# A SwiGLU block's gate and up products: weights as the moving operand, with a block scheme of seven products for eight over halves of the contraction

## The chip, the cores and the metric

The kernel runs on one core of one Trainium2 chip. The metric is the device time of one execution in microseconds (us). The kernel before takes 2006.88 us, the median of three runs (2005.92 to 2008.11). All arrays are fp32 in DRAM.

## What is computed

One inference step of a backbone layer over 128 context tokens and 256 latent tokens with D = 2048 channels: a modulation from a conditioning vector (six vectors of 2048, each for two conditions), a mixing sub-layer, and a SwiGLU feed-forward network (FFN) with 5632 hidden units. The change touches the FFN and what lies around it:

```
mod = silu(cond) @ w_ada + b_ada          # six vectors; ga2 is the last ("modulation 5")
...
h  = rmsnorm(x, norm_pre_ffn) * (1 + sc2) + sh2
ff = (silu(h @ w_ffn_gate) * (h @ w_ffn_up)) @ w_ffn_down
x  = x + ga2 * rmsnorm(ff, norm_post_ffn)
```

h is 384 tokens x 2048, gate and up are 2048 x 5632, down is 5632 x 2048.

## The kernel before

**Numbers.** Every fp32 operand is split into two parts, hi (a cast to the matmul's fp32r format) and lo (the difference), and a product takes three matmuls: w_hi x_hi, w_lo x_hi, w_hi x_lo. An operand is on chip as a pair of tiles: whi and wlo for weights, A_hi and A_lo (`h2`) for h, hid_hi and hid_lo for the hidden units.

**Weights.** A weight arrives in pieces of 512 KB, 128 partitions x 1024. SyncE (SP) issues the load into one of two buffers `raw` (L1307) or into four resident buffers `uraw` (tiles u012 and u3s, L1301). `split_next` (L1318) lets ScalarE (ACT) cast it to whi (L1324) and VectorE (DVE) subtract for wlo (L1325). There are four buffers each of whi and wlo. The list `ready` holds three pieces ahead of TensorE; `grab2` (L1336) takes the first, issues loads (`load_more`, L1289), splits one more piece, and issues one deferred VectorE operation out of the list `pend` (two in the last chunk).

**The FFN.** It goes through 11 chunks of 512 hidden units, `FC` = 4 column tiles each. Per chunk, gate and up take 16 pieces: `proj2` (L1374) takes two pieces for a column tile of 128, with the weights as the stationary operand and h as the moving one, 384 columns (`gemm`, L277; 24 matmuls a piece, 384 in a chunk). SiLU of gate is ScalarE's (L1349), the product with up VectorE's (L1356, tile hfE), and hid is split by `split_act` (L303, L304). The hidden units so stand with channels on partitions, which is how the down product needs them as its stationary operand.

The down product of chunk c runs inside chunk c + 1, in two halves (`down`, L1391). w_d is the moving operand, 512 columns. Per half, the context tokens are multiplied plainly and the latent tokens by a scheme of seven products for eight on blocks of 2 x 2: VectorE forms sums of four pieces of w_d (`combine`, L1312) and of hid (L1362 to L1367, once in a chunk), and TensorE makes 66 matmuls (`wmm`, L1386), 132 in a chunk. Nine partial results of 512 columns per half are added into fp32 sums in SBUF (psums, `unit`), L1408, by copies of ScalarE in the first chunk (L1406). In the last chunk the down product is plain (kind "e", tile pde).

**PSUM.** Two pools hold one bank (128 x 512) per buffer: psm with three ("mm"), used by gate and up, and pss with five ("side"), used by down.

**Modulation 5.** `ada_rest` (L563) works through w_ada for one modulation: per half of its columns, 16 loads of 512 KB (adaw, two buffers), each followed by a multiply (L573) or multiply-add (L575) on VectorE for each of two conditions, 1024 columns; then eight small matmuls (pr, L583), a copy by ScalarE (adev, L588), two transposes (ptm, L592) and small VectorE operations. It is a generator; `paced` and `step` let it take 0.25 of a step at each piece of gate and up, and what remained before the last piece would be finished there (L1478).

**The tail.** For the last norm, `add_last` (L1442) adds the last sums and squares them with a sum per token. `diagonal` (L1492) puts the factors 1/rms on a diagonal for each of three token tiles; `turn` (L1508, matmul L1512) turns blocks of f by a matmul with that diagonal, which scales and transposes at once; then x1 + ga2 x f is formed (L1537, or L1529 and L1530) and stored.

**What sets the order.** Each engine executes its instructions in the order in which the program emits them, and waits at one whose inputs or buffer are not ready. The lists above (`ffn_order`, `pend`, `ready`) and the pace of the modulation decide that order; the pools put the waits.

Of the kernel before, what the change touches and what calls it, by code (L numbers as in the profile page):

```python
# [96 lines left out]
def tile_step(ctx: ExitStack, tc: tile.TileContext, a, o):  # L97
# [74 lines left out]
    ffn_order = []  # L172
    for c in range(NFC):
        for j in range(FC):
            ffn_order.append(("g", c, j))
            if c and j == FC - 1 and c < NFC - 1:
                ffn_order.append(("d", c - 1, 1))
            ffn_order.append(("u", c, j))
            if c == NFC - 1 and j == FC - 1:
                ffn_order.append(("d", c - 1, 1))  # L180
            if c and j == 1:
                ffn_order.append(("d", c - 1, 0))
    ffn_order += [("e", NFC - 1, n) for n in (0, 2, 1, 3)]
# [5 lines left out]
    def ffn_srcs(kind, c, j):  # L189
        if kind == "d":  # L190

            return [("U", 0, down_src(c, j, 0)), ("U", 1, down_src(c, j + 2, 0)), ("U", 2, down_src(c, j + 2, 1)),
                    ("U", 3, down_src(c, j, 1)), ("T", 0), ("T", 1), ("T", 2), ("T", 3)]
        if kind == "e":
            return [("E", down_src(c, j, kh)) for kh in range(2)]
        return two(a["w_" + kind], c * FC + j)

    first = [ffn_srcs(*u) for u in ffn_order[:HEAD]]
    srcs += [f[g] for g in range(2) for f in first]
    ffn_items = []  # L200
    for u in ffn_order[HEAD:]:
        ffn_items += ffn_srcs(*u)

    plain = 2 * (2 * FC - HEAD)
    srcs += ffn_items[:plain]
    ffn_items = ffn_items[plain:]
# [834 lines left out]
    with ExitStack() as s:  # L1041
# [3 lines left out]
            pe.tile([P, FC, T], F32R, tag=f"hid_{n}", name=f"hid_{n}") for n in ("hi", "lo")  # L1045
        )
        pd_stack = s.enter_context(ExitStack())
# [39 lines left out]
        spare_h = ((pe, "hid_hi", 2), (pe, "hid_lo", 2))  # L1087
        spare_w = ((adap, "adaw", 2), (adap, "adaw", 2))
        raw2 = None
        for i in range(KT):  # L1090
            p = psm.tile([P, T], F32, tag="mm", name="pmm")
            for g in range(2):
# [3 lines left out]
                else:  # L1096
# [9 lines left out]
                    if -4 <= n <= -2:  # L1106
                        split(spare_w if n == -3 else spare_h)
# [150 lines left out]
        for q in range(2):  # L1258
# [10 lines left out]
        chi = actp.tile([P, 3, G], F32, tag="C_hi", name="u012")  # L1269
        clo = actp.tile([P, 3, G], F32, tag="C_lo", name="u3s")  # L1270
        uraw = [chi[:, 0], chi[:, 1], chi[:, 2], clo[:, 0]]
        S = [pf.tile([P, FC, TL], F32R, name=f"S_{n}") for n in ("hi", "lo")]
        units = [t[:, n, :] for t in (
            actp.tile([P, 6, 512], F32, tag="B_hi", name="psums"), actp.tile([P, 6, 512], F32, tag="B_lo", name="psums"),
            pf.tile([P, 2, 512], F32, name="psums2"),
        ) for n in range(t.shape[1])]
        units += [clo[:, 1 + n // 2, 512 * (n % 2) : 512 * (n % 2) + 512] for n in range(4)]

        def unit(j, x):

            return units[9 * j + x]

        entries, busy = list(raws), [False]
        raws.clear()
        entries = [("R", e[0]) for e in entries]
        items = [("R", src) for _, src in srcs] + [x if isinstance(x, tuple) else ("R", x) for x in ffn_items]
        pend, late_sums = [], [True]

        def load_more():  # L1289
            n = 0  # L1290
            while items and n < 3:
                it = items[0]
                if it[0] == "T":
                    entries.append(it)
                    items.pop(0)
                    continue
                if it[0] == "U":
                    if it[1] == 0 and busy[0]:
                        return
                    busy[0] = True  # L1300
                    SP.dma_start(uraw[it[1]].rearrange("p (i x) -> p i x", i=2), it[2])  # L1301
                    entries.append(("R", uraw[it[1]]))
                else:
                    if sum(e[0] == "R" and not any(e[1] is u for u in uraw) for e in entries) >= 2:
                        return
                    raw = wp.tile([P, G], F32, tag="raw", name="raw", bufs=2)
                    SP.dma_start(raw.rearrange("p (i x) -> p i x", i=2) if it[0] == "E" else raw, it[1])  # L1307
                    entries.append(("R", raw))
                items.pop(0)
                n += 1  # L1310

        def combine(n):  # L1312

            w11, w12, w22, w21 = uraw
            (lambda: DVE.tensor_sub(w22, w22, w12), lambda: DVE.tensor_sub(w12, w12, w11),  # L1315
             lambda: DVE.tensor_add(w11, w11, w22), lambda: DVE.tensor_sub(w21, w21, w11))[n]()  # L1316

        def split_next():  # L1318
            if not entries:
                return  # L1320
            e = entries.pop(0)
            raw = e[1] if e[0] == "R" else uraw[(2, 1, 0, 3)[e[1]]]
            hi, lo = (wp.tile([P, G], F32R, tag=t, name=t, bufs=4) for t in ("whi", "wlo"))
            ACT.copy(hi, raw)  # L1324
            DVE.tensor_sub(lo, raw, hi.bitcast(F32))  # L1325
            ready.append((hi, lo))

            if raw is uraw[2] and e[0] == "R":
# [293 lines left out]
```

## Time and profile before

| | |
|---|---|
| Median of three runs | 2006.88 us (2005.92 to 2008.11) |
| The profiled execution: its own time | 2006.71 us |
| its span in the profile | 2004.9 us |
| Instructions in the span | 29287 |
| FFN in the span, from the first matmul of gate and up (L1246) to the last of w_d | 906.0 to 1987.6 us |

The profiled execution's time exceeds its span by what lies before the first and after the last instruction of the trace. Busy time of TensorE is given for matmuls (PE) and for loading the stationary operand (PEld) apart, and overlaps between neighbours. A row of the timeline gives start, length, engine, line, operation and tiles; a row of waits gives who waited for whom, the sum in us, how many times and the mean; a row of the windows gives the stretch, its length, busy time with the count for PE, PEld, DVE, ACT and POOL, then the granted TensorE clock, the share of DMA and GB/s; a row of DMA gives the tile and its source, the queue, the count, the size and the median us from issue to landing; a row of groups gives line, engine, operation, tiles, shapes and count, then busy us and mean ns, then idle time before.

### The profile page before, as it was taken

To read this page: it belongs to the slowest core of one execution; us is meant where nothing else is said; L and a number is where in the kernel's file an instruction comes from. 1 tells how busy PE (TensorE), PEld (TensorE's weight loads), DVE (VectorE), ACT (ScalarE), POOL (GpSimd) and SP (SyncE) were. 2 spreads that over 40 slices of the span, in tenths; PEclk is the share of its full clock that TensorE was granted. 3 is DMA by queue.
4 is the path that set the end of the run, shared out by engine and by line. 5 is a ranking of instruction groups with operands and counts; after the bars stand their busy time and mean duration, and the time that the engine had idled before them with its cause. 6 is when DMAs were issued, how large, how long until landed. Compare 5 with 4: busy or idle time off the path is not lost.

```text
span 2004.9 us, 29287 instructions
## 1 busy us (share of the span) xinstructions
PE 1987.6 (99%) x11652; PEld 1868.2 (93%) x11652; DVE 1481.5 (74%) x1887; ACT 852.7 (43%) x1220; POOL 32.2 (2%) x44
## 2 busy tenths in 40 slices
PE   8999999999999999999999999999999999999998
PEld 5779999999999999999999998989998989899997
DVE  5668798888667778867566868776868686767676
ACT  4233454544346554446344434343434333343333
POOL 0000000000000000003000000000000000000001
PEclk9999999999999999999999999999999999999999
DMA  9978677767646786645435353544444454434343
GB/s 389 370 246 272 218 254 247 231 219 253 221 158 201 241 291 196 200 158 204 154 117 177 126 168 127 168 126 147 148 147 157 137 168 133 156 102 156 113 161 126
DMA packets 124521, 380.18 MB, mean 190 GB/s; under 512 B 13788, under 2 KB 32412, under 8 KB 120032
## 3 DMA queue, kind: packets, MB, share of 16 engines
q1 hardware_dynamic: 123520, 377.13, 56.9%
q8 instruction: 91, 1.49, 0.3%
q10 hardware_dynamic: 864, 1.18, 0.2%
q14 instruction: 46, 0.38, 0.1%
HBM read 361.48 MB, written 16.78 MB: 189 GB/s over the span
## 4 chain that ended last, share of the span: by engine, by line
PE 85%; DVE 11%; issue 2%; ACT 2%; DMA 1%; POOL 0%; DVEq 0%; ACTq 0%; POOLq 0%
PE pmm L277 64%; PE pdn L1386 5%; DVE wlo L1325 5%; PE pv L418 3%; DVE psums L1408 2%; PE pf L277 2%; PE pde L1386 2%; PE pgm L401 1%; ACT whi L1324 1%; PE px L436 1%; DVE u3s L1316 1%; PE pmm L1246 1%; DVE u L1315 1%; DVE adacc L575 1%; DMA raw<-in_w_g 1%
## 5 line engine op out<-in xcount | busy, mean ns | idle before, releaser
L277 PE MATMUL pmm<-A_hi,whi 128*128 128x384 f32 x2480 | 833.2, 336 | 0.0
L277 PE MATMUL pmm<-A_hi,wlo 128*128 128x384 f32 x2480 | 832.0, 335 | 0.0
L277 PE MATMUL pmm<-A_lo,whi 128*128 128x384 f32 x2480 | 830.1, 335 | 0.0
L277 PEld LDWEIGHTS pmm<-A_hi,wlo 128*128 128x128 f32 x2480 | 465.8, 188 | 4.3 <-DVE wlo L1325 4.3
L277 PEld LDWEIGHTS pmm<-A_hi,whi 128*128 128x128 f32 x2480 | 466.0, 188 | 3.8 <-issue 1.4
L277 PEld LDWEIGHTS pmm<-A_lo,whi 128*128 128x128 f32 x2480 | 465.9, 188 | 1.0
L1325 DVE TENSOR_TENSOR wlo<-raw,whi 128x1024 fp32r<-128x1024 f32 x175 | 214.2, 1224 | 214.4 <-ACT whi L1324 214.4
L1324 ACT CAST whi<-raw 128x1024 fp32r<-128x1024 f32 x175 | 183.1, 1052 | 310.9 <-DMA raw<-in_w_g 146.6
L575 DVE SCALAR_TENSOR_TENSOR adacc<-adaw,spad,adacc 128x1024 f32<-128x1024 f32 x240 | 297.1, 1279 | 0.7 <-DMA adaw<-in_w_ada 0.4
L243 ACT CAST whi<-raw 128x1024 fp32r<-128x1024 f32 x181 | 189.9, 1052 | 197.4 <-DMA raw<-in_w_gate 78.2
L244 DVE TENSOR_TENSOR wlo<-raw,whi 128x1024 fp32r<-128x1024 f32 x179 | 218.0, 1222 | 69.5 <-ACT whi L243 69.0
L1325 DVE TENSOR_TENSOR wlo<-u,whi 128x1024 fp32r<-128x1024 f32 x120 | 144.6, 1221 | 37.4 <-ACT whi L1324 36.9
L1324 ACT CAST whi<-u 128x1024 fp32r<-128x1024 f32 x120 | 125.0, 1050 | 75.5 <-PE pdn L1386 28.7
L1386 PE MATMUL pdn<-wlo,hid_hi 128*128 128x512 f32 x280 | 111.3, 398 | 3.2 <-DVE wlo L1325 2.8
L1386 PE MATMUL pdn<-whi,hid_lo 128*128 128x512 f32 x280 | 109.7, 392 | 0.0
L1386 PE MATMUL pdn<-whi,hid_hi 128*128 128x512 f32 x280 | 109.2, 390 | 0.0
L1408 DVE TENSOR_TENSOR psums<-psums,pdn 128x512 f32<-128x512 f32 x126 | 83.7, 682 | 0.0
L303 ACT CAST hid_hi<-hfE 128x384 fp32r<-128x384 f32 x44 | 22.6, 514 | 131.8 <-DVE hfE L1356 131.8
L1386 PEld LDWEIGHTS pdn<-wlo,hid_hi 128*128 128x128 f32 x280 | 52.6, 188 | 20.0 <-DVE wlo L1325 10.0
L1386 PEld LDWEIGHTS pdn<-whi,hid_hi 128*128 128x128 f32 x280 | 52.6, 188 | 11.0 <-ACT sg L1349 0.4
L1386 PE MATMUL pdn<-whi,S_hi 128*128 128x512 f32 x160 | 62.4, 390 | 0.0
L1386 PE MATMUL pdn<-wlo,S_hi 128*128 128x512 f32 x160 | 62.4, 390 | 0.0
(327 smaller groups left out, 2182.7 us busy)
## 6 DMA issues: line engine op xcount, KB each, us to landing
adaw<-in_w_ada SPq DMA_DIRECT2D x128, 512.0 KB, 4.1
raw<-in_w_g SPq DMA_DIRECT2D x88, 512.0 KB, 4.4
raw<-in_w_u SPq DMA_DIRECT2D x88, 512.0 KB, 4.5
slab<-in_w_ada SPq DMA_DIRECT2D x32, 1024.0 KB
raw<-in_w_gate SPq DMA_DIRECT2D x64, 512.0 KB, 4.5
u<-in_w_d SPq DMA_DIRECT2D x60, 512.0 KB, 4.4
raw<-in_w_in SPq DMA_DIRECT2D x44, 512.0 KB, 3.6
raw<-in_w_out SPq DMA_DIRECT2D x32, 512.0 KB, 4.5
```

What stands on the lines that cost most here:

```text
L243: ACT.copy(hi, raw)
L244: sub = lambda: eng.tensor_sub(lo, raw, hi.bitcast(F32))
L277: PE.matmul(dst, w[wi][:, k * n + n0 : k * n + n0 + P], x[xi][:, k0 + k, :], start=first and k == 0 and j == 0, stop=last and k == kts - 1 ...
L303: ACT.copy(hi, src)
L401: PE.matmul(pgv[q : q + 32, :], spad[:, k, :], slab[k // (KT // 2)][:, k % (KT // 2), :], start=k < 4, stop=k >= KT - 4,)
L418: PE.matmul(pv[2 * t + g], hT[x_][:, kb, t * P : (t + 1) * P], w_[:, g * 512 : (g + 1) * 512], start=kb == 0 and j == 0, stop=kb == KT - 1 ...
L436: PE.matmul(px, w_[:, u * P : (u + 1) * P], hT[x_][:, kb, :], start=j == 0, stop=j == 2)
L575: DVE.scalar_tensor_tensor(acc[:, c, :], w, spad[:, k, c : c + 1], acc[:, c, :], op0=ALU.mult, op1=ALU.add,)
L1324: ACT.copy(hi, raw)
L1325: DVE.tensor_sub(lo, raw, hi.bitcast(F32))
L1386: PE.matmul(dst, stat[x_][:, m, :], w[w_].rearrange("p (i k c) -> p i k c", i=2, k=2)[:, :, m, :], start=first and m == 0 and n == 0, stop ...
L1408: DVE.tensor_add(unit(j, x), unit(j, x), pt[x])
```

## The change

Chunk 0 keeps gate and up as they were. From chunk 1 on (chunks 2 to 11 in the words of the change), gate and up have the weights as the moving operand, in pieces of 256 rows of the contraction by 512 columns (all four column tiles; 1 KB contiguous per row of the source), and 128 tokens x 128 rows of h as the stationary one. The three token tiles t = 0 (context), 1 and 2 (latent) are the rows of the output. The context is multiplied plainly; the latent tokens go by seven block products for eight, with the halves of the contraction and gate against up as the two block indices of the weights. The schedule of a chunk is a list of steps, four of each kind:

- **A** (up, first half of the contraction) and **B** (gate, first half) read eight resident buffers (tiles u012, u345, u67), loaded up to a chunk ahead. A makes p1 and q1, B p5 and q3.
- **C** (gate, second half) arrives in `raw`, makes q3 and p3; VectorE forms from it and the resident pieces the sums that **E** (p6) and **F** (p7) use.
- **G** (up, second half) arrives in `raw`, makes q2 and p2; **H** (p4) uses another such difference.
- **D** is w_d, now plain: eight steps for each chunk, the first four between the E's, the other four behind the H's, three token tiles each. Its banks come from psm.

A step takes one piece from `ready`; a product over a piece takes six matmuls of 512 columns. A sums operation (`sum1`, or the differences in `split_next`) stands beside the splits. The ten partial banks (`banks`, from pss) are read by `evict`; hid now comes out with tokens on partitions (g0, g1, s5), and `turn_hid` transposes it into hid's layout, 12 transposes a chunk: token tiles 0 and 1 behind step A1 of the next chunk, tile 2 behind A2, in banks of psm. `left_sums` forms the sums of h once, during chunk 0. `grab2` now issues everything in `now` and two of `pend`.

Modulation 5 becomes `ada_last`: four quarters of 512 columns, loads of 256 KB into two halves of one buffer (w5), sums in acc5. It steps at 0.8 in A, G and the last four D's, and before its small matmuls (in psm) it yields as long as `pend` is not empty or a D has its banks. What remains is finished in one loop behind step D3 of the last chunk but one's w_d (the last lines below).

In the tail, f is scaled by 1/rms first (`scale`, on ScalarE, VectorE and GpSimd), then turned by plain transposes.

```diff
+        def left_sums():
...
+            h11, h12, h21, h22 = ([f(x) for x in Hx(t, k)] for t, k in ((1, 0), (1, 8), (2, 0), (2, 8)))
...
+        for c in range(1, NFC):
+            steps += [("A", c, i) for i in range(4)] + [("B", c, i) for i in range(4)]
+            for i in range(4):
+                steps += [("C", c, i), ("E", c, i), ("D", c - 1, i)]
+            for i in range(4):
+                steps += [("F", c, i), ("G", c, i), ("H", c, i)] + ([("D", c - 1, 4 + i)] if c < NFC - 1 else [])
+        steps += [("D", NFC - 2, 4 + i) for i in range(4)]
+        d_order = (0, 2, 1, 3)
+        steps += [("D", NFC - 1, 2 * n + k) for n in d_order for k in range(2)]
+        def gu_src(kind, c, half, i):
+            return a["w_" + kind][FC * c : FC * c + FC, half, :, 256 * i : 256 * i + 256].rearrange("n p x -> p n x")
...
+        def load_more(kept=1):
+            while pairs and out_now[0] < 2:
...
+            while kept and resident:
...
+        def sum1(c, i):
+            x, y = (slots[slot(n, c, i)] for n in range(2))
+            DVE.tensor_sub(x, y, x)
...
         def split_next():
...
+            kind, c, i, raw = entries.pop(0)
+            x, y = (slots[slot(n, c, i)] if kind not in "RD" else None for n in range(2))
+            src = raw if kind in "RCGD" else y if kind == "F" else x
             hi, lo = (wp.tile([P, G], F32R, tag=t, name=t, bufs=4) for t in ("whi", "wlo"))
+            ACT.copy(hi, src)
+            if (kind, i) == ("A", 3):
+                sum1(c, 0)
+            elif kind == "B" and i < 3:
+                sum1(c, i + 1)
+            elif kind == "C":
+                DVE.tensor_sub(x, raw, x)
+                DVE.tensor_sub(y, raw, y)
+            elif kind == "G":
+                DVE.tensor_sub(x, raw, x)
+            DVE.tensor_sub(lo, src, hi.bitcast(F32))
...
+        def grab2(kept=2):
             w = take()
+            while now:
+                now.pop(0)()
+            load_more(kept)
             split_next()
+            for _ in range(2):
                 if pend:
                     pend.pop(0)()
             return w
+        def ada_last():
+            m = 5
+            acc, wt = (adap.tile([P, 2, 512], F32, tag="adaw", name=n, bufs=2) for n in ("acc5", "w5"))
+            for q in range(4):
+                for k in range(KT):
+                    w = wt[:, k % 2, :]
+                    SP.dma_start(w, a["w_ada"][m - 2, q // 2, k, :, 512 * (q % 2) : 512 * (q % 2) + 512])
...
+                    yield
+                while pend or d_live[0]:
+                    yield
+                pr = psm.tile([P, P], F32, tag="mm", name="pr")
...
+                while pend or d_live[0]:
+                    yield
+                pt = psm.tile([P, P], F32, tag="mm", name="ptm")
+                PE.transpose(pt, ev, ident)
...
+        def products(w, todo, by_tile=False):
+            order = [(x, y) for x in ((0, 1),) for y in todo] if by_tile else [((0,), y) for y in todo] + [((1,), y) for y in todo]
+            for ws, (dst, stat, mov, first, last) in order:
+                for w_ in ws:
+                    for m in range(2):
+                        for x_ in range(2 - w_):
+                            PE.matmul(
+                                dst, stat[x_][m], mov(w[w_], m),
+                                start=first and w_ == m == x_ == 0, stop=last and w_ == m == 1,
+                            )
...
+        of_kind = {
+            "A": (("p1", Hx(1, 0), True, True), ("q1", Hx(0, 0), True, True)),
+            "B": (("p5", S1, True, True), ("q3", Hx(0, 0), True, False)),
+            "C": (("q3", Hx(0, 8), False, True), ("p3", S4, True, True)),
+            "E": (("p6", S2, True, True),),
+            "F": (("p7", S3, True, True),),
+            "G": (("q2", Hx(0, 8), True, True), ("p2", Hx(1, 8), True, True)),
+            "H": (("p4", Hx(2, 8), True, True),),
+        }
...
+        def evict(c, kind):
...
+            if kind == "A":
+                now.extend([lambda: ACT.copy(s1, B["p1"]), lambda: ACT.copy(sq, B["q1"])])
+            elif kind == "B":
+                now.append(lambda: ACT.copy(s5, B["p5"]))
+            elif kind == "C":
+                pend.extend([lambda: add(g0, sq, B["q3"]), lambda: add(g1, s5, B["p3"]), lambda: silu(g0)])
...
+        def turn_hid(dst, t, pool, tag):
+            pt = pool.tile([P, FC, P], F32, tag=tag, name="ptr")
+            src = (g0, g1, s5)[t]
+            for j in range(FC):
+                PE.transpose(pt[:, j, :], src[:, j * P : (j + 1) * P], ident)
+            hi, lo = (x[:, :, t * P : (t + 1) * P] for x in dst)
+            pend.extend([lambda: ACT.copy(hi, pt), lambda: DVE.tensor_sub(lo, pt, hi.bitcast(F32))])
...
+        rate[0] = 0.8
+        ada = paced(ada_last(), rate)
...
+                if kh == 0:
+                    while pend:
+                        pend.pop(0)()
+                    pool, tag = (pss, "side") if last_c and done % 2 else (psm, "mm")
+                    pd_tiles = [pool.tile([P, 512], F32, tag=tag, name="pdn") for _ in range(3)]
+                    d_live[0] = True
...
+                products(w, todo, by_tile=last_c and kh == 1)
+                if kh == 1:
+                    if not last_c:
+                        d_live[0] = False
+                        for t in range(3):
+                            if c == 0:
+                                pend.append(lambda u=unit(t, n), p=pd_tiles[t]: ACT.copy(u, p))
+                            else:
+                                pend.append(lambda u=unit(t, n), p=pd_tiles[t]: DVE.tensor_add(u, u, p))
...
+                if i == 3:
+                    evict(c, kind)
+                if kind == "A" and c > 1 and i in (1, 2):
+                    for t in ((0, 1), (2,))[i - 1]:
+                        turn_hid(hid, t, psm, "mm")
+                if kind in "AG":
+                    step(ada)
+            if (kind, c, i) == ("D", NFC - 2, 3):
+                while pend:
+                    pend.pop(0)()
+                for _ in ada:
+                    pass
...
+            PE.transpose(py[k][:, t * P : (t + 1) * P], unit(t, k // 4)[:, (k % 4) * P : (k % 4 + 1) * P], ident)
+        scale(DVE, 0, 0)
+        scale(DVE, 0, 1)
...
+        scale(POOL, 1, 3)
```

More of the change, by code (lines that the diff above doesn't have):

```diff
@@ L1277, in tile_step @@
[L1277 to L1283, printed above, removed]
-        raws.clear()
[L1285 to L1316, printed above, removed]
+        slots = [t[:, n, :] for t, k in (
+            (actp.tile([P, 3, G], F32, tag="C_hi", name="u012"), 3), (actp.tile([P, 3, G], F32, tag="C_lo", name="u345"), 3),
+            (adap.tile([P, 2, G], F32, tag="adacc", name="u67"), 2),
+        ) for n in range(k)]
@@ new lines, in tile_step @@
+        raws.clear()
+        pairs = []
+        for _, src in srcs:
+            entries.append(["R", 0, 0, None])
+            pairs.append((entries[-1], src))
+        for kind, c, i in steps:
+            e = [kind, c, i, None]
+            entries.append(e)
+            if kind in "CGD":
+                pairs.append((e, src_of(kind, c, i)))
+        resident = [(kind, c, i) for c in range(1, NFC) for kind in "AB" for i in range(4)]
+        out_now = [sum(e[3] is not None for e in entries)]
@@ L1369, in tile_step @@
+            DVE.tensor_mul(hf, ep[j % 2][:, 0:T], p)
+            split_act(hid[0][:, j, :], hid[1][:, j, :], hf)
         dst_of = {"g": gate_dst, "u": up_dst}
@@ L1372, in tile_step @@
             dst_of[kind](hp[u], c, j)
[L1374 removed]
+        n = 0
+        for kind, c, j in ffn_order[HEAD:]:
             p = psm.tile([P, T], F32, tag="mm", name="pmm")
             for g in range(2):
[L1377 to L1389 removed]
```

365 lines of the change are left out of this document (189 added, 176 removed).

## Prediction

> **What bounds the kernel now.** First the page of the profile: the span, TensorE's share, the chain.
>
> ```profile
> span 2004.9 us, 29287 instructions
> ...
> PE 1987.6 (99%) x11652; PEld 1868.2 (93%) x11652; DVE 1481.5 (74%) x1887; ACT 852.7 (43%) x1220; POOL 32.2 (2%) x44
> ...
> PE 85%; DVE 11%; issue 2%; ACT 2%; DMA 1%; POOL 0%; DVEq 0%; ACTq 0%; POOLq 0%
> ```
>
> TensorE (PE) is never free and most of the chain is its own, so an edit is worth what it does to TensorE's stream. Durations of matmuls overlap; what counts is start to start, from the timeline of PE, first and last of a run each time: 43 intervals at 512 columns, 40 at 384, and the final turns (128 columns, plain fp32) in one row.
>
> ```profile
> 1403.31 0.39 PE L1386 MATMUL pdn<-whi,hid_lo 128*128 128x512 f32 x1
> ...
> 1413.06 0.39 PE L1386 MATMUL pdn<-whi,hid_hi 128*128 128x512 f32 x1
> ...
> 1416.93 0.34 PE L277 MATMUL pmm<-A_hi,wlo 128*128 128x384 f32 x1
> ...
> 1423.86 0.34 PE L277 MATMUL pmm<-A_hi,whi 128*128 128x384 f32 x1
> ...
> 1989.86 6.52 PE L1512 MATMUL py<-dg,psums 128*128 128x128 f32 x56 [0.19 <-DVE dg L1494]
> ```
>
> So 0.2267 us, 0.1733 us and 0.116 us. The length of a chunk comes from one VectorE (DVE) line that runs once in each (instructions of the tile hfE), its slack from a stretch of 100 us, and PE's waits from the waits of PE's loads after 960 us.
>
> ```profile
> L1362 DVE TENSOR_TENSOR hfE<-hfE x10: 424/425/426, 975.6 to 1862.1; 128x256 f32<-128x256 f32 x10
> ```
>
> ```profile
> 1210.00:1310.00 100.00, 98.95 (x523) 91.82 (x522) 76.47 (x81) 37.47 (x42) 0.00 (x0) 1.00 0.46 148
> ```
>
> ```profile
> PEld pdn L1386 <- DVE wlo L1325: 10.2, 17, 1.1
> PEld pmm L277 <- DVE wlo L1325: 4.3, 17, 0.3
> ```
>
> A chunk takes (1862.1 - 975.6) / 9 = 98.5 us; its stream is 384 x 0.1733 + 132 x 0.2267 = 96.5 us. VectorE is busy 76 us of 100, and TensorE waits only some 15 us for it in the whole FFN. The FFN is bound by TensorE with little slack on VectorE.
>
> **The change: TensorE's stream.** For c = 1 to 10 the 384 matmuls of gate and up become 11 products x 6 matmuls x 4 slices = 264 of 512 columns; the 132 of w_d become 144; and 12 turns are added. 408 x 0.2267 + 12 x 0.116 = 93.9 us against 96.5: -2.6 us a chunk, **-25.5 us** in ten. The 2.0 us by which a chunk exceeds its stream are partly waits on wlo behind the sums of w_d, which go: between 0 and -20 us; I take **-12**, what the two rows of waits mostly hold.
>
> **VectorE.** Prices, start to start, from its timeline; ScalarE's cast from the page:
>
> ```profile
> 1488.61 1.22 DVE L1325 TENSOR_TENSOR wlo<-u,whi 128x1024 fp32r<-128x1024 f32 x1
> 1489.74 2.47 DVE L575 SCALAR_TENSOR_TENSOR adacc<-adaw,spad,adacc 128x1024 f32<-128x1024 f32 x2
> 1492.13 1.22 DVE L1325 TENSOR_TENSOR wlo<-u,whi 128x1024 fp32r<-128x1024 f32 x1
> ...
> 1504.47 2.35 DVE L1325 TENSOR_TENSOR wlo<-u,whi 128x1024 fp32r<-128x1024 f32 x2
> 1506.74 1.28 DVE L1408 TENSOR_TENSOR psums<-psums,pdn 128x512 f32<-128x512 f32 x2
> 1507.93 1.22 DVE L1325 TENSOR_TENSOR wlo<-u,whi 128x1024 fp32r<-128x1024 f32 x1
> ```
>
> ```profile
> L1324 ACT CAST whi<-raw 128x1024 fp32r<-128x1024 f32 x175 | 183.1, 1052 | 310.9 <-DMA raw<-in_w_g 146.6
> ```
>
> 1024 wide (a wlo or a difference) 1.13 us; 512 wide 0.60; the multiply-add of the modulation 1.195 at 1024, so 1.195 - 0.53 = 0.66 at 512 (an estimate from these rows), a pair 1.3. A chunk now has 36 wlo, 16 differences, 27 of 512: 58.8 + 16.2 = 75 us, and up to ten pairs, 88 us, below 93.9: VectorE does not bound on the whole. But TensorE waits for it in places, and these I read from the order of the new program's instructions and what each waits for.
>
> Place 1: **the turns of hid in step A1** (c = 2 to 10). They come in TensorE's queue behind A1's matmuls and go to the three psm buffers that D's last three sums held. The second turn is released by the sum of D's tile 1, and in VectorE's queue that sum stands behind wlo of B1. There are four buffers of whi and wlo and three are ahead, so wlo(A3) can't start before D's last matmul has read its buffer. Take that end as 0. VectorE then does wlo(A3), two 512, a difference, wlo(B0), two 512, a difference, wlo(B1), one 512: 5 x 1.13 + 5 x 0.60 = 8.65 us, with starts and hand-overs 8.9. TensorE arrives after A0, A1 and four turns: 24 x 0.2267 + 0.46 = 5.9. Everything of A2 is queued behind the turn. So **3.0 us** a chunk, where no multiply-adds lie between (c = 3, 4, 7, 8). In c = 5 and 10 four pairs lie there, in 6 and 9 three: counted from wlo(A0), which starts 0.7 us after step G3 (7.4 us before 0), 9 x 1.13 + 10 x 0.60 + 8 x 0.66 = 21.5, so the gate opens at 14.3: **8.4 us**; with three pairs 7.1. In c = 2 the sums are copies by ScalarE behind its cast of B1 (1.05 us by its row): about 2. Sum 2 + 4 x 3.0 + 2 x 8.4 + 2 x 7.1 = **+45 us**; between 25 (VectorE half as late) and 60.
>
> Place 2: **the rest of the modulation.** It is paced by 0.8 at steps A, G and late D, but waits while anything is pending, and the order shows the last quarter, 16 pairs, in one block behind D(9,3), with its eight small matmuls on TensorE ahead of F(10,0). So TensorE stands through all of it; the splits that are ready don't help. w5 has two halves: a load goes out when the pair two earlier is done. What a load takes, by the DMA view (of 1110 to 1810 us, and of the end):
>
> ```profile
> adaw<-in_w_ada SPq DMA_DIRECT2D x22, 512.0 KB, 3.7
> ```
>
> ```profile
> gate<-gates_d SPq DMA_DIRECT2D x32, 192.0 KB, 3.9
> ...
> out_yT<-x1b ACTq DMA_DIRECT2D x6, 192.0 KB, 2.6
> ```
>
> And the prices of what stands around the pairs, from the groups of instructions after 940 us:
>
> ```profile
> L573 DVE TENSOR_SCALAR adacc<-adaw,spad 128x1024 f32<-128x1024 f32 x4 | 2.8, 749 | 0.0
> ...
> L583 PE MATMUL pr<-adacc,selr 128*32 128x256 f32 x32 | 2.1, 385 | 0.0
> ...
> L592 PE MATMUL ptm<-ident,adev 128*128 128x128 f32 x4 | 0.8, 270 | 0.0
> L588 ACT COPY adev<-pr 128x256 f32<-128x256 f32 x2 | 0.7, 373 | 1.1 <-PE pr L583 1.1
> ```
>
> 256 KB lies between 192 and 512 KB: 2.8 us by the line through 2.6 and 3.7, and 3.9 at most. Two pairs then take 2.8 + 0.1 + 1.3 = 4.2; seven such 29.5; the first two pairs 0.8 (half of 749 ns, twice) + 1.3 = 2.1. Ahead stand the third quarter's three sums (1.8), matmuls (0.4), copy (0.4) and transpose (0.3), 3.0 us; behind, matmuls, copy and transpose again, 1.1, and as much for hand-overs, 2.1. **+37 us**; 26 at VectorE's own pace (15 x 1.3 + 0.8 + 5), 45 with loads of 3.9 us. Before, such operations lay singly in VectorE's slack and their last one started at 1737 us:
>
> ```profile
> L575 DVE SCALAR_TENSOR_TENSOR adacc<-adaw,spad,adacc x240: 1275/1279/1292, 158.1 to 1737.2; 128x1024 f32<-128x1024 f32 x120
> ```
>
> After a pause the clock matters. The granted clock, and busy counts, by windows, and TensorE's last row:
>
> ```profile
> 4.00:8.00 4.00, 3.84 (x6) 2.19 (x7) 0.71 (x2) 3.47 (x8) 0.00 (x0) 1.00 1.00 407
> 8.00:14.00 6.00, 6.00 (x17) 3.37 (x16) 5.97 (x13) 5.08 (x12) 0.00 (x0) 1.00 1.03 418
> ...
> 2000.00:2004.90 4.90, 0.00 (x0) 0.00 (x0) 0.00 (x0) 0.00 (x0) 0.00 (x0) 0.86 0.56 198
> ```
>
> ```profile
> 1998.67 0.39 PE L1512 MATMUL py<-dg,u3s 128*128 128x128 f32 x2
> ```
>
> The first matmuls take 0.64 us, later ones 0.35: half speed for about 6 us from the start. At the end 0.86 means half speed for 1.4 us, so the clock fell at about 2003.5, some 4.5 us after the last matmul. So +3 after place 2; in place 1 the pauses are 4.6 us at most, and I count nothing. The Trainium skill's page "TensorE: Matmul & The Clock Gate", section "What's actually happening", halves the clock after an idle window of about 3.4 us and restores it after as much work: then each of the four chunks with pairs would lose some 1.7 us more. No row here shows a pause that short.
>
> Small ones, together **+3** (0 to 6). Before the last D the hid is turned, cast and split, and the last tile's part has nothing to cover it:
>
> ```profile
> L304 DVE TENSOR_TENSOR hid_lo<-hfE,hid_hi 128x384 fp32r<-128x384 f32 x43 | 24.0, 558 | 24.9 <-ACT hid_hi L303 24.9
> ...
> L303 ACT CAST hid_hi<-hfE 128x384 fp32r<-128x384 f32 x43 | 22.1, 514 | 131.2 <-DVE hfE L1356 131.2
> ```
>
> At 384 columns cast and difference take 1.1 us, at 512 some 1.5. The tail scales twelve blocks where three diagonals were made, on three engines at once, another 1.5. Nothing for the sums of h at c = 0: 14 wide operations, 14 x 1.13 = 16 us, in VectorE's slack there, 13.6 us of the last 26 of chunk 0 and as large a share of the 19 before; without it, 16.
>
> ```profile
> 950.00:976.00 26.00, 26.00 (x152) 26.00 (x151) 12.40 (x13) 6.93 (x9) 0.00 (x0) 1.00 0.55 179
> ```
>
> Nothing for loads in pieces of 1 KB: no row has them in the FFN. Pieces of 4 KB and of 2 KB land alike:
>
> ```profile
> raw<-in_w_g SPq DMA_DIRECT2D x56, 512.0 KB, 4.4
> u<-in_w_d SPq DMA_DIRECT2D x45, 512.0 KB, 4.4
> ```
>
> A load has from wlo two loads earlier to its own step, some 6.8 us; late by 1 us each, 80 loads would cost 80, which I hold improbable.
>
> **Sum.** -25.5 - 12 + 45 + 37 + 3 + 3 = +50.5 us on the execution profiled, 2006.7 us (span 2004.9, 0.2 below the median of 2006.88): **2057 us**.
>
> **Rivals.**
> 1. The gates of place 1 open in time. For it: ready weights lie three steps ahead and VectorE has 19 us of slack a chunk. Against: its queue is in order and the sum stands behind wlo(B1). Without the 45: 2012 us.
> 2. Pauses of place 1 halve the clock, twice a chunk with pairs, 3 us each by the row of the start: +24, 2081 us. For it: 4.6 us against the 4.5 of the end. Against: turns lie between.
> 3. Faster: TensorE's own stream decides, because VectorE reaches what TensorE stands before in time, the block of place 2 too. Price: -25.5 - 12 + 3 = -34.5, 1972 us. It decides the sign only if all waits together stay below 34.5 us, of 85 counted; the block alone at VectorE's pace has 26. Against: the multiply-adds can't precede their loads.
> 4. The change doesn't do what it says: the order shows all 2640 and 1584 matmuls at 512 columns. 2007 us.
>
> **Numbers.** The forecast with its bounds 0.72; rival 1 0.10; rival 2 0.10; rival 3 0.07; rival 4 0.01. The range 2030 to 2083 takes in the forecast's bounds that don't all fall together and rival 2, and leaves out 1, 3 and 4. Differences below 0.2% can't be told from no change here; faster 0.07, same 0.02 (rival 4 and a part of 1), slower 0.91.
>
> **What would show it.** PE busy falls from 99%; at turns of hid idle time released by VectorE's psums line, 3 us without and 7 to 8 us with multiply-adds; one pause near 37 us in the last chunk, released by a multiply-add, which itself waits for in_w_ada; between turns, a chunk near 94 us of stream. It is wrong if that pause is missing or short, if the turns wait below 1 us, or if pgu matmuls are paced otherwise than 0.227 us.

## The result, and the profile after

| | before | after |
|---|---|---|
| median | 2006.78 us (2005.92 to 2008.11, 4 runs) | 2094.74 us (2092.76 to 2096.18, 4 runs) |
| ratio, 95% interval | | 1.0437 (1.0419 to 1.0455) |
| span of the profiled execution | 2004.9 us | 2094.4 us |

The changed kernel is 88 us slower. The sign was forecast; the size (+50) was not, and the time lies above the range of 2030 to 2083 us. The page of the changed kernel, its span, busy times and chain:

```profile
span 2094.4 us, 27765 instructions
...
PE 1980.6 (95%) x10676; PEld 1744.8 (83%) x10676; DVE 1628.7 (78%) x2048; ACT 903.6 (43%) x1261; POOL 33.2 (2%) x44
...
PE 83%; DVE 10%; DMA 4%; ACT 2%; issue 2%; SPq 0%; POOL 0%; DVEq 0%; ACTq 0%; POOLq 0%
```

TensorE has lost 7 us of busy time and gained 97 us of idle time (2004.9 - 1987.6 = 17 before, 2094.4 - 1980.6 = 114 now). Where the idle time lies, the waits of PE's matmuls say, from chunk 2 to the last product (who waited for whom, the sum, how many times, and the longest single wait, not the mean, as was said of these rows above):

```profile
PE ptr L1524 <- DVE psums L1576: 40.7, 16, 4.7
PE pr L1415 <- DVE acc L1406: 31.1, 1, 31.1
PE pdn L1463 <- DVE psums L1576: 18.7, 9, 5.6
PE ptr L1524 <- ACT psums L1574: 2.3, 1, 2.3
...
PE ptm L1425 <- ACT adev L1420: 0.8, 2, 0.4
```

First and fourth row, 43.0 us, are the turns of hid in step A1. The second is the one block of the modulation. The third, 18.7 us, was in no term of the forecast: w_d's products wait for sums of w_d. With the small rows these are some 94 us; before, PE's matmuls waited 2.8 us from 960 us to the end of the FFN (the 15 us of the prediction are waits of its weight loads).

**Turns.** Chunk c = 3, without multiply-adds; PE, then VectorE, in the same microseconds:

```profile
1176.23 1.07 PE L1463 MATMUL pgu<-wlo,A_hi 128*128 128x512 f32 x4
1178.03 0.66 PE L1524 MATMUL ptr<-ident,ep 128*128 128x128 f32 x4 [0.73 <-DVE psums L1576]
1180.89 0.66 PE L1524 MATMUL ptr<-ident,ep 128*128 128x128 f32 x4 [2.21 <-DVE psums L1576]
```

```profile
1177.29 0.68 DVE L1576 TENSOR_TENSOR psums<-psums,pdn 128x512 f32<-128x512 f32 x1
1177.89 1.22 DVE L1353 TENSOR_TENSOR u<-u,u 128x1024 f32<-128x1024 f32 x1
1179.02 1.22 DVE L1372 TENSOR_TENSOR wlo<-u,whi 128x1024 fp32r<-128x1024 f32 x1
1180.15 1.28 DVE L1576 TENSOR_TENSOR psums<-psums,pdn 128x512 f32<-128x512 f32 x2
```

The first sum frees a bank at 1177.97 and the first turn starts; the second sum stands behind a difference and a wlo and ends at 1180.8, and the second turn starts at 1180.89. VectorE is never idle in between: it does, in order, what it was given.

**The block.** PE, and the loads of w5 in that stretch:

```profile
1959.70 0.61 PE L1463 MATMUL pdn<-wlo,hid_hi 128*128 128x512 f32 x2
...
1961.65 0.33 PE L1425 MATMUL ptm<-ident,adev 128*128 128x128 f32 x1 [0.39 <-ACT adev L1420]
1993.05 1.22 PE L1415 MATMUL pr<-acc,selr 128*32 128x128 f32 x16 [31.07 <-DVE acc L1406]
...
1994.84 0.77 PE L1463 MATMUL pgu<-whi,A_hi 128*128 128x512 f32 x1
```

```profile
w<-in_w_ada SPq DMA_DIRECT2D x14, 256.0 KB, 2.6
```

**The third row.** Step D4 of chunk 2's w_d; PE's third token tile and VectorE beside it:

```profile
1239.84 0.39 PE L1463 MATMUL pdn<-whi,hid_lo 128*128 128x512 f32 x1
1241.54 0.50 PE L1463 MATMUL pdn<-whi,hid_hi 128*128 128x512 f32 x1 [1.31 <-DVE psums L1576]
```

```profile
1236.19 1.23 DVE L1372 TENSOR_TENSOR wlo<-u,whi 128x1024 fp32r<-128x1024 f32 x1 [1.64 <-ACT whi L1362]
1237.34 1.28 DVE L1576 TENSOR_TENSOR psums<-psums,pdn 128x512 f32<-128x512 f32 x2
1238.53 1.22 DVE L1371 TENSOR_TENSOR u<-raw,u 128x1024 f32<-128x1024 f32 x1
1239.67 1.22 DVE L1372 TENSOR_TENSOR wlo<-raw,whi 128x1024 fp32r<-128x1024 f32 x1
1240.80 0.68 DVE L1576 TENSOR_TENSOR psums<-psums,pdn 128x512 f32<-128x512 f32 x1
```

It is the turns' mechanism at another place. D4 takes the three psm banks of D2 and D3; two of their sums go by themselves, the third stands behind a difference and a wlo. VectorE even had 1.64 us to spare just before.

**The clock.** Windows in c = 3 around the pause's longer part, in c = 7 over the same pause, and after the block (the column behind the five engines is the granted clock):

```profile
1178.15:1181.57 3.42, 1.21 (x9) 0.97 (x10) 3.42 (x5) 0.00 (x0) 0.00 (x0) 1.00 0.00 0
1181.57:1184.98 3.41, 3.41 (x9) 2.67 (x9) 1.00 (x1) 0.04 (x1) 0.00 (x0) 0.50 0.02 5
1184.98:1188.39 3.41, 3.41 (x18) 2.77 (x18) 1.83 (x2) 1.49 (x2) 0.00 (x0) 1.00 0.00 0
1594.58:1598.00 3.42, 2.04 (x11) 1.22 (x9) 3.42 (x5) 1.05 (x1) 0.00 (x0) 1.00 0.00 0
1598.00:1601.41 3.41, 1.86 (x10) 1.63 (x11) 3.23 (x4) 0.00 (x0) 0.00 (x0) 1.00 0.00 0
1994.00:2000.00 6.00, 5.56 (x27) 4.31 (x20) 3.95 (x6) 2.76 (x4) 0.00 (x0) 0.72 0.00 0
```

The same pause is followed by half clock and 9 matmuls in 3.41 us in c = 3, and by full clock in c = 7. The windows are steps of the grid on which this trace's clock changes: its thirteen stretches at half clock with work in them all start and end on one grid of 3.41 us, and are 1, 2, 3 or 10 steps of it long. In c = 3 the idle stretch of 2.21 us lies whole in one step, with 1.21 us of work, and the next step has half the clock. In c = 7 a boundary (1598.00) cuts it in two; both steps have 1.86 us of work or more, and the clock stays. In this trace, from 960 us to the end of the FFN, every step at full clock with 1.93 us of idle time or more was followed by half clock, and none with 1.86 or less. In other runs the grid lies elsewhere against the program, so it is partly chance which pauses cost. The forecast had taken 4.5 us as the length of a pause from which the clock falls. At the end of the kernel before, the last matmul ends at 1999.1 and the clock falls at 2003.5: between them lie the rest of a step that still had 2.4 us of work and one whole idle step, so 4.5 us was a delay and no threshold.

**The balance.** The work with hardly a wait is e13_best below, with as many instructions of TensorE and a span of 1971.1 us: 33.8 below the kernel before. From there to 2094.4 are 123.3 us: 94 are idle time of TensorE (114 against 20), as much as the rows above hold, and 29 are busy time (1980.6 against 1951.2). Of these 29, some 25 are the clock. The sum over the twelve stretches at half clock from 960 us on:

```profile
sum 98.99, PE 50.31 PEld 39.51 DVE 68.77 ACT 10.44 POOL 1.15; mean PE 4.19 PEld 3.29 DVE 5.73 ACT 0.87 POOL 0.10
```

TensorE works 50.3 us in them, and does half as much as it would at full clock (9 matmuls against 18 above). In e13_best the clock is 1.00 from 960 to 1955 us.

### The profile page after: what moved, and what is told of

It is laid out like the page before. It is cut to its first block, busy times and chain, and to the rows that moved or that the text cites. A ratio compares the mean times of both kernels' runs of the same rounds, so it can differ in the third digit from the quotient of the medians.

```text
span 2094.4 us, 27765 instructions
## 1 busy us (share of the span) xinstructions
PE 1980.6 (95%) x10676; PEld 1744.8 (83%) x10676; DVE 1628.7 (78%) x2048; ACT 903.6 (43%) x1261; POOL 33.2 (2%) x44
## 4 chain that ended last, share of the span: by engine, by line
PE 83%; DVE 10%; DMA 4%; ACT 2%; issue 2%; SPq 0%; POOL 0%; DVEq 0%; ACTq 0%; POOLq 0%
PE pmm L252 30%; PE pgu L1463 26%; PE pdn L1463 16%; PE pv L393 3%; DVE wlo L1372 2%; PE pgm L376 1%; DMA raw<-in_w_in 1%; DVE acc L1406 1%; DVE u L1353 1%; PE px L411 1%; DVE psums L1576 1%; DMA w<-in_w_ada 1%; PE pmm L1222 1%; PE ptr L1524 1%; ACT whi L218 1%
## 5 line engine op out<-in xcount | busy, mean ns | idle before, releaser
L252 PE MATMUL pmm<-A_hi,whi 128*128 128x384 f32 x1200 | 404.2, 337 | 0.0
L252 PE MATMUL pmm<-A_hi,wlo 128*128 128x384 f32 x1200 | 401.3, 334 | 0.0
L252 PE MATMUL pmm<-A_lo,whi 128*128 128x384 f32 x1200 | 401.2, 334 | 0.0
L1463 PE MATMUL pgu<-whi,A_hi 128*128 128x512 f32 x640 | 258.2, 403 | 0.0
L1463 PE MATMUL pgu<-whi,A_lo 128*128 128x512 f32 x640 | 255.7, 399 | 0.0
L252 PEld LDWEIGHTS pmm<-A_hi,whi 128*128 128x128 f32 x1200 | 225.3, 188 | 2.5 <-issue 1.4
L252 PEld LDWEIGHTS pmm<-A_lo,whi 128*128 128x128 f32 x1200 | 225.4, 188 | 0.2
L252 PEld LDWEIGHTS pmm<-A_hi,wlo 128*128 128x128 f32 x1200 | 225.3, 188 | 0.0
L1463 PE MATMUL pdn<-whi,hid_hi 128*128 128x512 f32 x480 | 190.5, 397 | 19.4 <-DVE psums L1576 18.7
L1463 PE MATMUL pgu<-wlo,A_hi 128*128 128x512 f32 x640 | 186.1, 393 | 0.0
L1463 PEld LDWEIGHTS pgu<-whi,A_hi 128*128 128x128 f32 x640 | 124.3, 194 | 26.2 <-issue 0.4
```

Of the source, the lines that this page charges most:

```text
L252: PE.matmul(dst, w[wi][:, k * n + n0 : k * n + n0 + P], x[xi][:, k0 + k, :], start=first and k == 0 and j == 0, stop=last and k == kts - 1 ...
L1463: PE.matmul(dst, stat[x_][m], mov(w[w_], m), start=first and w_ == m == x_ == 0, stop=last and w_ == m == 1,)
```

## Experiments

Times without an interval are one execution; executions of the runs with an interval differ by up to 6 us.

**e1_no_mod5** leaves out modulation 5's sums.

```diff
-        ada = paced(ada_last(), rate)
+        POOL.memset(mods[:, 5], 1.0)
+        ada = paced(iter(()), rate)
```

> Leaves out modulation 5's sums (its values are set to one), so its loads, multiply-adds and small matmuls are gone. Theory: the block behind step D3 of the last chunk but one's w_d costs 36 us, and the pairs lengthen the wait at A1's turns in c = 5, 6, 9, 10 from 3.2 us to 8 to 9, another 20, plus 3 of half clock and of D4 in c = 5: about 2036 us. Rival, the pairs only fill VectorE's slack and A1's wait is the same with and without them: 2058 us.

Measured 2023.02 us, and PE's waits:

```profile
PE ptr L1524 <- DVE psums L1577: 23.5, 16, 2.2
PE pdn L1463 <- DVE psums L1577: 15.3, 9, 4.8
```

The block is gone, the turns fall from 43.0 to 24 us (another row has 0.3), the waits for D's banks by 3. Modulation 5 thus costs 31 + 19 + 3 us of waits. What is left of the 72 us, some 18, is busy time, and most of it the clock: TensorE works 19.7 us at half clock here from 960 us on, 50.3 in the changed kernel, which makes 15 us. The theory (2036) had 3 us for that. The rival (2058) is out.

**e2_sums_first** changes one position in a list.

```diff
-                                pend.append(lambda u=unit(t, n), p=pd_tiles[t]: DVE.tensor_add(u, u, p))
+                                pend.insert(t, lambda u=unit(t, n), p=pd_tiles[t]: DVE.tensor_add(u, u, p))
```

> The sums of w_d go to the front of the list of deferred operations instead of its end; no work is added or removed. Theory, VectorE's order decides when the psm banks come free: the waits at A1 without pairs (3.2 us) and those in D4 (1.5 us and more, 20 in all) vanish, those at A1 with pairs shrink by about 4.7 us each, and the half clock at A2 (11 us) goes with them: about 2035 us. Rival, VectorE's total load or the number of banks decides: waits move elsewhere and the time stays at 2085 to 2095 us.

Measured 2045.26 us.

```profile
PE pr L1415 <- DVE acc L1406: 30.9, 1, 30.9
PE ptr L1524 <- DVE ep L1514: 16.8, 9, 4.3
PE pdn L1463 <- DVE psums L1576: 7.0, 1, 7.0
PE ptr L1524 <- DVE ep L1517: 5.1, 7, 1.5
```

With the same work on VectorE the eight waits in D4 are gone (the 7.0 is one wait, in D6 of the last chunk but one). No turn waits for a sum any more; those that still wait do so for g1 and s5 (tile ep), which have taken the sums' place at the queue's end. The order decides, not VectorE's load. The run lacks 10 us to the theory: that had left some 15 us at the turns with pairs (8 to 9 less 4.7, four times), where 22 are left, and D6's wait was to go with those in D4.

**e3_turn_in_B** puts the turns four steps later.

```diff
-                if kind == "A" and c > 1 and i in (1, 2):
+                if kind == "B" and c > 1 and i in (1, 2):
```

> The turns of hid are emitted four steps later, behind B1 and B2 instead of A1 and A2; no work is added or removed. Theory, TensorE arrives before the gate opens at 9 to 14 us after D's end and would now arrive at 14 to 16: the 49 us at A1 and the 11 us at A2 vanish, D4's 20 us and the block's 36 stay: about 2035 us. Rival, VectorE's load or the banks decide: the wait moves to B1 and the time stays near 2095 us.

Measured 2016.17 us, 19 less than the theory gave.

```profile
PE pdn L1463 <- DVE psums L1576: 21.0, 10, 5.1
PE pdn L1463 <- DVE hid_lo L1526: 6.6, 4, 2.0
```

```profile
L1415 PE MATMUL pr<-acc,selr x64: 272/273/297, 1174.0 to 1870.2; 128*32 128x128 f32 x64
```

The turns do not wait at all, as forecast; D's banks cost as before, and hid is now at times late for D0 (6.6 us, not foreseen). But the block's row is missing too: the last of the modulation's small matmuls starts at 1870.2 us, in step A of the last chunk. With the turns at another place the list of deferred operations empties at steps where the modulation asks, so hardly anything is left for a block. This run undid two things.

**e5_mod5_spread** lets the small matmuls go in step B.

```diff
-                while pend or d_live[0]:
-                    yield
+                held[0] = True
+                yield
                 pr = psm.tile([P, P], F32, tag="mm", name="pr")
...
+                if kind == "B" and held[0] and not pend:
+                    next(ada_gen, None)
```

> Modulation 5 no longer yields until nothing is pending: its small matmuls go into step B as soon as the list is empty, so all four quarters are done by step B1 of chunk c = 9 and no block is left behind D3. No work is added or removed. Theory: the block's 36 us go, but pairs now lie in A1's queue in eight chunks instead of four, at 5 to 6 us each, and none in c = 10: 36 down, 17 up, 2076 us. Rival, the pairs' work costs the same wherever it lies (VectorE's load): 2090 to 2095 us; rival, the wait at A1 does not depend on pairs: 2058 us.

Measured 2067.8 us.

```profile
PE ptr L1523 <- DVE psums L1576: 34.2, 16, 3.4
PE pdn L1462 <- DVE psums L1576: 24.9, 9, 5.3
```

The block is gone; before D4, 6 us more are waited. The turns wait 36.5 us (with a row of 2.3 for c = 2), 6.5 less and not 17 more: pairs lie ahead of A1 in every second chunk only, since a quarter that waits for step B lets the steps A before it pass without pairs.

**e6_fill** and **e10_fill_h** put matmuls of no use into A1's pause; the first repeats A1's product, the second (whose edit is shown) uses h alone:

```diff
+                if kind == "A" and c > 1 and i == 1:
+                    for m in range(16):
+                        PE.matmul(bank[c, "p5"][:, 0:T], h2[0][:, 0, 0:P], h2[0][:, m, :], start=m == 0, stop=m == 15)
```

> Adds work of no use: behind A1 in c = 2 to 10 twelve matmuls into a bank that B0 starts anew, 2.7 us of TensorE that lie inside its wait at the turns; 108 matmuls, 24 us of busy time. Theory, the pauses at A1 halve the clock afterwards: pauses of 3.2 us shrink to 0.5 and the slow A2 behind them (1.6 us each in c = 2 to 4) goes, those with pairs shrink from 8 or 9 to 6 us and still halve: 5 us faster than the changed kernel, 2088 to 2091 us. Rival, the slow A2 is no matter of the clock: no gain, 2095 us. Rival, the added work is not covered: 24 us more, 2119 us.

> The changed kernel with 16 matmuls of no use behind A1 in c = 2 to 10, now on h alone (384 columns, 2.8 us), so that no weight buffer is held longer; they lie inside the wait at A1's turns. Theory, pauses there halve the clock: without pairs 3.2 us of pause become 0.4 and the slow A2 behind them goes (1.6 us in c = 2, 3, 4), with pairs the pause stays at 5 to 6 us and halves the clock as before: 5 us faster than the changed kernel, 2088 to 2091 us, though 25 us of work are added. Rival, the clock has no part in it and the work is covered: 2095 us. Rival, the work is not covered: 2119 us.

e6_fill took 2101.17 us (2098.52 to 2102.99). It was badly made: its matmuls read A1's weights, so the buffer came free later and the gate moved back with them: in c = 3 the second turn starts 10.9 us after A0's first matmul, 9.2 in the changed kernel. e10_fill_h took 2088.59 us (2083.83 to 2089.63), 6 us less than the changed kernel with 25 us more work, as the theory of the clock has it: the turns wait 20.5 us instead of 43.0, and TensorE works 34.5 us at half clock from 960 us on instead of 50.3, which is worth 8. Windows of the pause in c = 3 and behind it:

```profile
1178.60:1181.30 2.70, 2.34 (x13) 1.95 (x13) 2.11 (x3) 0.00 (x0) 0.00 (x0) 1.00 0.00 0
1179.40:1182.40 3.00, 3.00 (x16) 2.42 (x15) 1.31 (x2) 0.76 (x1) 0.00 (x0) 1.00 0.00 0
```

The clock stays at 1.00 and A2 runs at 16 matmuls in 3 us.

**e7_order** has e2's edit, and the turns behind A3 and B0.

```diff
-                if kind == "A" and c > 1 and i in (1, 2):
-                    for t in ((0, 1), (2,))[i - 1]:
+                if c > 1 and (kind, i) in (("A", 3), ("B", 0)):
+                    for t in ((2,), (0, 1))[kind == "A"]:
```

> Two edits of order: the sums of w_d at the front of the deferred operations, and the turns behind A3 (two tiles) and B0 (the third). The list then empties earlier, so the modulation's quarters go by themselves and one round of its small matmuls is left behind D3. Theory: of the changed kernel's waits only x1b's loads (9 us), the small matmuls (3 to 4) and the turns themselves are left: 1978 to 1984 us, faster than before. Rival, VectorE at 80 us of 100 bounds with its pairs, and waits return at D0 or in step A: 2005 us or more.

1998.31 us (1997.74 to 1998.63), 0.9959 of the kernel before (0.9944 to 0.9974): faster by 0.4%, but 14 to 20 us above the forecast. A new wait had appeared, for pieces that arrive late:

```profile
PEld pdn L1463 <- ACT whi L1362: 12.6, 5, 3.5
```

It comes five times, up to 3.5 us, always ahead of the third D step: w_d's piece is cast late, because ScalarE's cast ahead of it waits for w_gate's. D6's wait is left too (5.1 us).

**e8_late_x1b** adds to e7's edits a move of the text of x1b's loads, **e9_spread** adds e5's edit to it.

```diff
-                x1b = actp.tile([P, KT, T], F32, tag="A_hi", name="x1b")
...
+                    if last_c and done == 2:
+                        x1b = actp.tile([P, KT, T], F32, tag="A_hi", name="x1b")
```

> The two edits of order, and x1b's four loads issued at the third pair of the last w_d steps, behind the last weight, instead of ahead of the first. Theory, these loads take DMA time from w_d's last pieces and cost 8 to 9 us: that much below the run with the two edits alone, 1970 to 1976 us. Rival, the last pieces are late anyhow, because only two are in flight: no difference; rival, x1b is then late for the tail: slower by up to 8 us.

> As the run before, and modulation 5's small matmuls in step B, so that nothing of it is left behind D3. Theory: 3 to 4 us less than without (its last small matmuls and copies are covered): 1967 to 1973 us. Rival, pairs in one more chunk make new waits: same or up to 5 us more.

e8_late_x1b took 1997.61 us (1996.87 to 1999.72), as e7_order. SyncE's queue says why it tells nothing:

```profile
1920.78 0.46 SPq L1563 DMA_DIRECT2D x1b<-x_d  x1
1923.27 0.37 SPq L1339 DMA_DIRECT2D raw<-in_w_d  x1
1923.69 0.46 SPq L1563 DMA_DIRECT2D x1b<-x_d  x1
```

The loads still alternate with w_d's: on SyncE the program's scheduler had put them where their buffer comes free, not where the text has them: the last matmul that reads the buffer's earlier content starts at 1920.2 us (the sentence above that each engine follows the text does not hold for this queue). e9_spread took 1989.72 us (1988.81 to 1990.97), 8 less than without the spread, more than the 3 to 4 forecast; its forecast time, 1967 to 1973 us, rested on a gain of e8 that did not come.

**e12_x1b_held** and **e14_pss** build on e9_spread, for the wait in D6 of the last chunk but one. The first holds x1b's loads back, the second takes D6's banks from the other pool; its x1b loads stand in the text where the changed kernel has them, which e8 showed to make no difference.

```diff
+                            DVE.tensor_copy(x1b[:, 4 * q, 0:1], ssq[:, 0, 0:1])
                             SP.dma_start(x1b[:, 4 * q : 4 * q + 4, :], x1_d[:, 4 * q : 4 * q + 4, :])
```

```diff
-                    pool, tag = (pss, "side") if last_c and done % 2 else (psm, "mm")
+                    pool, tag = (pss, "side") if last_c and done % 2 or (c, i) == (NFC - 2, 6) else (psm, "mm")
```

> The run e9_spread with x1b's four loads held back: a column of each part is first written by VectorE from the squares of the last chunk's first sums, so that the loads can only follow all loads of w_d. In e8_late_x1b the loads had stayed where they were in SyncE's queue, so that run told nothing. Theory, x1b's 3 MB take DMA time from w_d's pieces, and the sums of step D5 wait in VectorE's queue behind the split of a late piece: the 6.2 and 1.5 us of waits after D5 and D6 go, 1980 to 1983 us. Rival, two pieces in flight are too few anyhow: 1989 to 1990 us.

> The run e9_spread with one edit: step D6 of the last chunk but one's w_d takes its three banks from pss instead of psm, so that it does not wait for the sums of D4 and D5. x1b's loads lie as in the changed kernel. Theory after e12_x1b_held: D6's wait is for banks, because those sums stand in VectorE's queue behind the split of a piece that was loaded just then, and x1b has no part in it: the 6.2 us go, 1983 to 1984 us. Rival, the pieces of w_d are late in any case (two in flight): 1989 to 1990 us.

e12_x1b_held: 1990.09 us (1988.72 to 1993.40), no gain, though the loads now stand behind all of w_d's. e14_pss: 1986.87 us (1982.33 to 1988.00), some 3 of the 6 us. The wait had gone to the next user of those banks:

```profile
PE ptr L1523 <- DVE psums L1576: 3.2, 1, 3.2
```

So D6 waits for banks, and x1b's loads by themselves are not its cause; half of it returned at the last turns.

**e13_best** has both, and steps the modulation at G, H and late D at a rate of 0.72.

```diff
-                if kind in "AG":
+                if kind in "GH" and not held[0]:
                     step(ada)
```

> e12_x1b_held with two more edits: modulation 5 steps at G, H and the last four D's at 0.72 instead of A, G, D at 0.8, so that no pairs lie in VectorE's queue ahead of the C steps; and the last pair's banks of the last chunk but one come from pss. Theory, in chunks with pairs ahead the loads of C and D start up to 6 us later and step E2 waits for them (8 us at E2, 4 at D2 in e9_spread); these go too: 1968 to 1974 us. Rival, two raw buffers bound the C, E, D steps whatever lies ahead: 1980 to 1983 us.

1973.50 us (1972.87 to 1974.03), 0.9833 of the kernel before (0.9820 to 0.9846). Its page, and its longest waits of PE's matmuls:

```profile
span 1971.1 us, 27778 instructions
...
PE 1951.2 (99%) x10676; PEld 1728.8 (88%) x10676; DVE 1621.5 (82%) x2052; ACT 905.5 (46%) x1261; POOL 33.2 (2%) x44
```

```profile
PE py L1638 <- DVE psums L1629: 2.1, 3, 1.1
PE pdn L1462 <- DVE hidE L1525: 0.9, 1, 0.9
```

The number of PE's instructions is that of the changed kernel to the last one (10676). The waits ahead of the third D step, which e9_spread still had three times (2.3 to 2.6 us; behind E2, not at it as the expectation has it), are gone with the pairs ahead of them, so two raw buffers suffice when nothing delays their readers. That is shown for the edits together; no run has the new stepping alone.

## Why the prediction failed in size

1. **TensorE's stream, right.** 512 columns take 0.226 us also with h stationary (eight intervals below), and chunk 1, which has no turns, 92.5 us = 408 x 0.2267. The sum without waits was -34.5 us (rival 3, 1972 us); e13_best's span is 33.8 below the kernel before. That is the sum alone: no run has the term of -12 or the small ones apart.

```profile
975.14 0.39 PE L1463 MATMUL pgu<-whi,A_hi 128*128 128x512 f32 x1
...
1067.66 0.39 PE L1463 MATMUL pgu<-whi,A_hi 128*128 128x512 f32 x1
```

```profile
1233.83 0.39 PE L1463 MATMUL pgu<-whi,A_hi 128*128 128x512 f32 x1
...
1235.64 0.39 PE L1463 MATMUL pgu<-wlo,A_hi 128*128 128x512 f32 x1
```

2. **Place 1, right:** 43.0 us for 45, and not by luck: 0.73 + 2.21 = 2.9 us for 3.0 in c = 3, and in c = 5, 6, 9 and 10, where pairs lie ahead, 6.5 to 7.8 us for 7.1 to 8.4. That the queue's order makes it, e2 and e3 show; that pairs lengthen it, e1.
3. **Place 2, right:** TensorE stands from 1960.3 to 1994.8, 34.5 us, for 37; a load of 256 KB took 2.6 us for the 2.8 estimated. Its lower bound, 15 x 1.3 + 0.8 + 5, comes to 25 and not 26, which changes nothing.
4. **The step "they go to the three psm buffers that D's last three sums held" was applied to the turns alone.** Every second D step takes those banks as well. Their gates, D4 in eight chunks and D6 once, cost 18.7 us and were not in the sum. e2 removes D4's by order alone.
5. **The step "in place 1 the pauses are 4.6 us at most, and I count nothing" failed.** Pauses of 2 to 5 us did halve the clock, most of the time, and that cost some 25 us where the forecast had 3 for the block: 15 of them behind the turns, in seven of nine chunks (not in c = 7 and 8), the rest behind waits in D4, the block, D6 and in the tail. Rival 2 had +24, all at the turns with pairs; that its size is near is luck, since chunks without pairs and other places are in it. e10 shows the mechanism, and for c = 2 to 4 a part of the size. The Trainium skill's page "TensorE: Matmul & The Clock Gate", section "What's actually happening", lets a window of activity of about 3.4 us run free of the kernel's start, so that the moment of a change depends on where in it the work falls. The trace agrees: its grid has 3.41 us, and c = 3 and c = 7 differ by it. The same section of the Trainium skill lets the clock fall after an idle window. Here 1.93 us of idle time in a window sufficed, and the measurement decides. With the 18.7 us of point 4 and these 25, less the 3 counted, the forecast would have been 2098 us; measured are 2095.
6. **The range** took rival 2 and the forecast's bounds one at a time. Its upper end is the forecast with rival 2 and nothing else late; a second wait of the same kind had no room.
7. **Small terms, right in sum:** the half clock after the block cost 1.7 us (0.28 of 6) for 3; loads in pieces of 1 KB show in no wait of TensorE in the changed kernel.

What stays open: some 4 of the 29 us, and what the clock counts as work. In the tail, where TensorE does transposes, a step with only 1.55 us of idle time (2075.9 to 2079.3) was followed by half clock too.

## What to carry to other kernels

When a change puts a new user on a small pool of PSUM banks, list every user of that pool and, for each, what stands in the releasing engine's queue ahead of the release; the gate that you found is seldom the only one. Release first: the sums that free banks belong at the head of the deferred work, and the filler work (here multiply-adds) at steps after which no bank is awaited. The same instructions took 2094.7 us in one order and 1973.5 in another, with three banks taken from another pool and four small writes more, so a scheme that saves matmuls is judged only after its order. And price a pause of TensorE with the clock behind it: in c = 3 one of 2.9 us cost another 1.7.

## What the runs showed of the hardware beyond expectation

- A pause in two parts, 0.7 and 2.2 us, was followed by half clock in one chunk and by full clock in another: the clock went by steps of 3.41 us, and in the FFN it fell behind each with 1.93 us of idle time or more.
- TensorE with 25 us of matmuls of no use was 6 us faster than without (2088.59 against 2094.74 us), because they kept it busy in its pauses.
- VectorE was 82% busy over the span of the fastest kernel, and the waits that it gave TensorE in the FFN and the tail sum to some 4 us; at 78%, in the changed kernel, they were 93.
